# Attention stage of a two-layer trunk: q, k and v tiles paired otherwise, value products with 64 stationary columns, merge factors through DRAM, and the next MLP's first weight splits later

## The chip, the core and the metric

The program runs on one core of a Trainium2 chip. The core has a matrix engine (PE, whose weight loads are listed as PEld), a vector engine (DVE), a scalar engine (ACT), a general engine (POOL) and a queue engine (SP) that issues nearly all DMA transfers. The engines run their own instruction streams in order and wait for each other at semaphores. The metric is the device time of one execution in microseconds (us), lower is better; the kernel before takes 2144.97 us, the median of three runs (2143.05 to 2145.32).

## What is computed

One sequence of 1024 positions with 1024 features goes through two layers in float32. Layer 0 mixes positions with a gated unit in chunks of 128, layer 1 with dilated attention; a squared-ReLU MLP of width 4096 follows each, and norms stand before every block. Only the attention matters here:

```python
for g, (window, dil) in enumerate(((128, 1), (512, 4), (2048, 16))):   # three groups
    s = q_g k_g^T / 8 + bias, banded: a query sees keys t - j*dil, j = 0..window//dil
    m_g = max(s);  p = exp(s - m_g);  den_g = sum(p);  num_g = p @ v_g
m_all = max_g m_g;  c_g = exp(m_g - m_all)
o = sum_g(num_g * c_g) / sum_g(den_g * c_g)     # per head and position
h = h + o @ w_out
```

There are 8 heads of 64 features. The factor that multiplies num_g is c_g divided by the summed denominator: one number per head, position and group.

## The kernel before

**Arithmetic.** A float32 number is split in two parts (`hi`, made by an ACT copy to the float32r type, and `lo`, made by a DVE subtraction, both in `split` at L205 and L206). A product is then three matmuls, hi*hi, hi*lo and lo*hi. Large products use Strassen's scheme with seven block products, numbered 1 to 7 (`seven`, L1189), of 12 matmuls each.

**Stage.** The attention stage takes 36 column blocks of w_qkv, each of 128 columns (two heads): for four head pairs (hp) and three groups (g, in the order 1, 2, 0) a q, a k and a v tile. That makes twelve units U[0] to U[11]. Four tiles come out of a classical product at the start, (0,q), (0,k), (0,v) and (1,q). The other 32 are made in pairs by `seven`; the list `quads` says which two share one call. `put_out(i, s, ...)` hands over half s of the i-th tile of the pair: `out_qk` (L1156) for q and k, which it scales and splits to a hi and a lo tile (L1174 on ACT, L1175 on DVE), `out_v` for v.

**A unit.** For each of four query blocks j of a unit, PE makes scores (12 matmuls with 64 rows, the two heads side by side in the array), DVE adds the bias and takes the maximum (L1270), ACT takes the exponential (L1272), PE transposes the probabilities (`turned`), ACT and DVE split them (L205, L206), and PE multiplies them by V (`values`). In `values` a head's V is 128 stationary columns, the 64 of the hi part beside the 64 of the lo part; two matmuls (by the hi and the lo part of the probabilities) give both halves of the bank, and an ACT copy (L1309) with a DVE addition (L1310) sums the halves into N.

**Merge.** When the third unit (g = 0) of a head pair has its scores for half i of the positions, `merge` computes the factors f on 128 positions x 3 groups x 4 blocks x 2 heads. For each group ACT spreads them over 128 columns per block (L1427), PE transposes them into a bank (`spread_factors`, 4 transposes), and DVE multiplies N by the bank (L1445 for groups 1 and 2, L1456 for group 0). For the first three head pairs the sum goes to DRAM and is read back near the end of the stage; the fourth is split and projected at once.

**What sets the order.** PE's order is the program's own. A planner (`Flow`) runs the projection as the main line, adds up PE time as it issues matmuls, and interleaves generators (attention, v tiles, merges) each of which says with `yield` how many ns later, or after which event, its next PE work is due; the table LAT holds those due times. `flow.until` stops the main line until an event has happened, so the generators' PE work then follows without projection products in between. In `out_qk` the first output of a k tile of unit i stops so until unit i-1 has issued its scores (its tiles need room). The other engines' orders come from a list scheduler, in which `tc.high_priority` pulls work forward.

**Around the end.** After the last pair, `project_three` and `project_last` multiply the merged outputs by w_out, covering the last unit's chain. The next MLP's first weights, `first = [plain(up(1, 0))]`, four loads and four splits of 128 x 512, are issued between the two calls of `project_three`.

Of the kernel before, what the change touches and what calls it, by code (L numbers as in the profile page):

```python
# [10 lines left out]
F32 = mybir.dt.float32  # L11
F32R = mybir.dt.float32r
AF = mybir.ActivationFunctionType
ALU = mybir.AluOpType
# [3 lines left out]
P = 128  # L18
# [89 lines left out]

LAT = dict(sum=2600.0, rms=2600.0, tile=1600.0, gate=8500.0, soft=4700.0, turn=4200.0, fe=1300.0, v=2000.0, qk=4000.0, merge=2600.0, out=700.0, fex=3.0, ve=1600.0)


@with_exitstack
def trunk(ctx: ExitStack, tc: tile.TileContext, xT, w_u, w_v, w_o, w_s, b_s, w_qkv, w_bo, rel,
# [1074 lines left out]

    def seven(w, x, more, put_out, begun=None, first=False):  # L1189

# [19 lines left out]
        if first:  # L1210
            a = one(1)
            u = copied(a)
            d = one(3)
            plus(u, one(6), u)
            one(2, a)
            put_out(0, 0, a)
            e = one(7)
            c22 = plus(u, e)
            f = one(5)
            put_out(1, 1, c22, f, True)  # L1220
            put_out(0, 1, plus(u, f), d, True)
        else:
            u = one(6)
            if begun:
                begun()
            u = copied(u)
            a = one(1)
            plus(u, a, u)
            d = one(5)
            c22 = plus(u, d)  # L1230
            e = one(7)
            put_out(1, 1, c22, e, True)
            one(2, a)
            put_out(0, 0, a)
            one(3, d)
            put_out(0, 1, u, d)
        one(4, e)
        put_out(1, 0, u, e, True)

    def geometry(g, j):  # L1240
# [7 lines left out]
        at = [0, keys[0][1] * P]  # L1248
        return keys, at, at[1] + keys[1][1] * P

    def scores(u, j):
# [11 lines left out]
        for hd in range(2):  # L1263
            p = temp()
            for i in range(2):
# [5 lines left out]
                                               scale=1.0, scalar=BIG, accum_out=m)  # L1271
                nc.scalar.activation(p[:, c], p[:, c], AF.Exp, bias=m, scale=-1.0, accum_out=dn)  # L1272
            ps.append(p)
# [15 lines left out]
    def values(u, j, pts):  # L1289
# [7 lines left out]
        for hd in range(2):  # L1297
            lst = list(parts.items())
            for n, (kb, cs) in enumerate(lst):
                pc, oc, w = cs[0][0], hd * 2 * P + cs[0][1], len(cs) * P  # L1300
                tv, at_ = place(u.g, kb)
                va = u.V[tv][:, at_, 2 * hd:2 * hd + 2, :]
                for e in range(2):
                    matmul(pv[:, oc:oc + w], va, pts[hd][e][:, pc:pc + w], start=(hd == 0 and n == 0 and e == 0),
                           stop=(n == len(lst) - 1 and e == 1), skip_group_check=True)
        for hd in range(2):
            r, x = slice(64 * hd, 64 * hd + 64), slice(64 - 64 * hd, 128 - 64 * hd)
            o, c = u.N[r, 2 * j * P:(2 * j + 2) * P], slice(hd * 2 * P, (hd + 1) * 2 * P)
            nc.scalar.activation(o, pv[x, c], AF.Copy)  # L1309
            nc.vector.tensor_tensor(o, o, pv[r, c], op=ALU.add)  # L1310

# [87 lines left out]
    def merge(hp, i):  # L1399
# [8 lines left out]
        nc.vector.tensor_tensor(mn, mn, e[2][:, :, :, 0], op=ALU.min)  # L1408
        f = small.tile([P, 3, 4, 2], F32, tag="f", name="f", bufs=2)
        for g in range(3):  # L1410
            nc.vector.tensor_tensor(f[:, g], mn, e[g][:, :, :, 0], op=ALU.subtract)
        nc.scalar.activation(f, f, AF.Exp)
        dn = small.tile([P, 4, 2], F32, tag="dn", name="dn", bufs=2)
# [6 lines left out]
        for g in range(3):  # L1420
            nc.vector.tensor_tensor(f[:, g], f[:, g], dn, op=ALU.mult)
        quick.__exit__(None, None, None)
        yield LAT["merge"]
        def factors(g):
# [12 lines left out]
        rest = None  # L1437
        fe_ns = LAT["fe"] * (1.0 if hp == 3 else LAT["fex"])
        early = {g: factors(g) for g in (1, 2, 0)} if hp == 3 else {}
        for g in (1, 2):  # L1440
            fe = early.get(g) or factors(g)
            yield fe_ns
# [5 lines left out]
            else:  # L1448
                nc.vector.tensor_tensor(rest, rest, t, op=ALU.add)
        fe = early.get(0) or factors(0)  # L1450
        yield fe_ns
# [6 lines left out]
        yield LAT["sum"]  # L1458
        if hp < 3:
            if i == 0:  # L1460
                kept_N[hp] = dram.tile([P, S], F32, tag=f"N{hp}", name=f"N{hp}", bufs=1)
            nc.sync.dma_start(kept_N[hp][:, half(i)], N)
        else:
            split_N(hp, i, N)
        merged[hp, i].t = flow.t
# [79 lines left out]
    for n, two in enumerate(quads):  # L1545
# [6 lines left out]
        seven(w, xa, more, lambda i, *x: out(two[i], *x), None if wn else lambda: flow.add(ahead_of_last()), n == 0)  # L1552
        w = wn
# [5 lines left out]
    for m in range(8):  # L1559
        project_three(0, m)  # L1560
    first = [plain(up(1, 0))]
    rest = list(range(8))
    while len(rest) > 4:
        project_three(1, rest.pop(0))
    for i in range(2):
        flow.until(lambda: (3, i) in outs)
        project_last(i, rest if i else ())
        start_terms(sq[i], i, 3, terms)
# [101 lines left out]
```

## Time and profile before

| | |
|---|---|
| median of three runs | 2144.97 us (2143.05 to 2145.32) |
| the profiled execution's own time | 2143.75 us |
| its span, from the first to the last instruction | 2142.0 us |
| PE busy | 2106.6 us, 98% |
| DVE busy | 1640.1 us, 77% |
| ACT busy | 1120.9 us, 52% |
| POOL busy | 566.1 us, 26% |
| mean granted TensorE clock | 0.994 |

Views of the trace give, per stretch of time, the busy time of each engine and the granted clock; per group of equal instructions, their number, busy time and mean duration; per wait, which engine waited for what. In a timeline row stand the start, the time from the first start to the last end, and the instructions with their count. A matmul's row lasts until its result is out, longer than the distance to the next matmul; the price of a matmul in a stream is therefore taken from the starts of rows that follow each other.

### The profile page before, as it was taken

Reading aid. Unit: us, or ns where it says so; the run is one execution under the profiler, and the core shown is the slowest. Engines: PE = TensorE matmul, PEld = TensorE weight load, DVE = VectorE, ACT = ScalarE, POOL = GpSimd, SP = SyncE. Lnnn points to the kernel's source line nnn. Section 1 sums busy time; section 2 is a strip of 40 time slices with the busy share of each in tenths; the row PEclk is TensorE's granted clock in tenths of the full one; section 3 lists DMA queues with packets and bytes.
Section 4 is the critical chain, followed back from the end, with each engine's and each line's share of the span. In section 5 each row is a group of like instructions: output and inputs, shape, how many; then the busy total and the mean of one; then the engine's idle time right before and its main releaser. Section 6 shows DMA issues by size and latency. Waiting matters only on the chain.

```text
span 2142.0 us, 30066 instructions
## 1 busy us (share of the span) xinstructions
PE 2106.6 (98%) x10210; PEld 1745.0 (81%) x10210; DVE 1640.1 (77%) x3014; ACT 1120.9 (52%) x2262; POOL 566.1 (26%) x417
## 2 busy tenths in 40 slices
PE   8999999999999999999999999999999999999998
PEld 7888887888878888887888788887888888888887
DVE  7975268567699888888787877879976666988886
ACT  6644136554564444346666656665555556544433
POOL 2100113233323332531212222101133332432345
PEclk9999999999999999998999999999999999999999
DMA  6411114455354444321112111142155543644432
GB/s 222 142 61 50 40 42 139 157 188 182 128 182 163 158 162 133 94 89 42 46 47 49 40 49 46 47 131 82 39 179 191 188 158 128 196 157 140 144 106 79
DMA packets 158815, 247.04 MB, mean 115 GB/s; under 512 B 33482, under 2 KB 47941, under 8 KB 158661
## 3 DMA queue, kind: packets, MB, share of 16 engines
q1 hardware_dynamic: 158336, 244.94, 35.2%
q8 instruction: 80, 1.31, 0.3%
q14 instruction: 75, 0.61, 0.1%
q10 hardware_dynamic: 324, 0.18, 0.0%
HBM read 180.41 MB, written 64.66 MB: 114 GB/s over the span
## 4 chain that ended last, share of the span: by engine, by line
PE 85%; DVE 9%; ACT 3%; issue 1%; DMA 1%; SPq 0%; DVEq 0%; ACTq 0%
PE at L180 43%; PE mm L180 40%; PE at L187 2%; DVE wp L206 2%; DMA t<-hid 1%; DVE h L340 1%; DVE t L206 1%; ACT t L1272 1%; ACT wp L205 1%; DVE k L1175 0%; DVE q L1175 0%; DVE tr L206 0%; DVE t L1270 0%; DVE N L1310 0%; ACT q L1174 0%
## 5 line engine op out<-in xcount | busy, mean ns | idle before, releaser
L205 ACT ACTIVATE wp<-r 128x512 fp32r<-128x512 f32 (+3 forms) x490 | 294.0, 605 | 455.5 <-PE at L180 287.2
L180 PE MATMUL at<-hx,wp 128*128 128x512 f32 x1770 | 413.7, 389 | 4.6 <-DVE wp L206 2.6
L206 DVE TENSOR_TENSOR wp<-r,wp 128x512 fp32r<-128x512 f32 (+3 forms) x490 | 375.9, 771 | 38.6 <-ACT wp L205 35.0
L180 PE MATMUL mm<-y,wp 128*128 128x512 f32 x1608 | 397.5, 393 | 2.2 <-ACT t L1132 1.0
L180 PEld LDWEIGHTS at<-hx,wp 128*128 128x128 f32 x1770 | 331.7, 188 | 75.8 <-DVE h L940 3.6
L180 PEld LDWEIGHTS mm<-y,wp 128*128 128x128 f32 x1608 | 298.7, 188 | 67.5 <-DVE h L340 1.6
L180 PE MATMUL at<-t,wp 128*128 128x512 f32 x1344 | 314.0, 389 | 0.1
L180 PEld LDWEIGHTS at<-t,wp 128*128 128x128 f32 x1344 | 252.2, 188 | 52.9 <-DVE t L803 0.5
L410 POOL TENSOR_TENSOR t<-r 128x512 f32<-128x512 f32 (+3 forms) x78 | 114.5, 1467 | 678.3 <-DMA r<-in_w_dn 312.7
L412 POOL TENSOR_TENSOR r<-r 128x512 f32<-128x512 f32 (+3 forms) x77 | 116.4, 1512 | 384.9 <-DVE wp L206 352.2
L180 PE MATMUL mm<-t,wp 128*128 128x512 f32 x768 | 195.1, 402 | 0.0
L206 DVE TENSOR_TENSOR hx<-t,hx 128x512 fp32r<-128x512 f32 x192 | 179.8, 949 | 5.7 <-ACT hx L205 5.7
L180 PE MATMUL mm<-hx,wp 128*128 128x512 f32 x708 | 171.7, 389 | 0.0
L180 PEld LDWEIGHTS mm<-t,wp 128*128 128x128 f32 x768 | 143.0, 191 | 30.9 <-issue 0.2
L269 POOL TENSOR_TENSOR t<-t 128x512 f32<-128x512 f32 (+1 forms) x54 | 72.8, 1347 | 347.8 <-ACT t L258 345.9
L180 PE MATMUL mm<-y,whi 128*128 128x512 f32 x512 | 158.1, 390 | 0.0
L180 PEld LDWEIGHTS mm<-hx,wp 128*128 128x128 f32 x708 | 132.7, 188 | 28.1 <-DVE b L966 0.6
L940 DVE TENSOR_TENSOR h<-h,at 128x512 f32<-128x512 f32 x144 | 97.6, 680 | 55.3 <-PE at L180 55.3
L803 DVE TENSOR_TENSOR t<-t,at 128x512 f32<-128x512 f32 x116 | 79.1, 683 | 76.6 <-PE at L180 76.4
L180 PE MATMUL at<-y,wp 128*128 128x512 f32 x552 | 137.5, 390 | 0.0
L205 ACT ACTIVATE hx<-t 128x512 fp32r<-128x512 f32 x192 | 118.4, 628 | 27.7 <-DMA t<-hid 23.3
L415 POOL TENSOR_TENSOR r<-r 128x512 f32<-128x512 f32 (+3 forms) x77 | 105.3, 1368 | 80.9 <-issue 47.1
(225 smaller groups left out, 3187.3 us busy)
## 6 DMA issues: line engine op xcount, KB each, us to landing
t<-hid SPq DMA_DIRECT2D x194, 256.0 KB, 4.9
hid<-t SPq DMA_DIRECT2D x140, 256.0 KB, 2.3
r<-in_w_up SPq DMA_DIRECT2D x128, 256.0 KB, 2.7
r<-in_w_dn SPq DMA_DIRECT2D x88, 256.0 KB, 2.7
r<-in_w_qkv SPq DMA_DIRECT2D x72, 256.0 KB, 2.6
hid<-b SPq DMA_DIRECT2D x56, 256.0 KB, 2.7
r<-in_w_v SPq DMA_DIRECT2D x48, 256.0 KB, 3.6
h<-in_xT SPq DMA_DIRECT2D x16, 256.0 KB, 4.1
```

Source lines behind the costliest of these rows:

```text
L180: nc.tensor.matmul(out, lhsT, rhs, **kw)
L187: nc.tensor.transpose(out, src, ident)
L205: nc.scalar.activation(hi, src, AF.Copy)
L206: nc.vector.tensor_tensor(lo, src, hi.bitcast(F32), op=ALU.subtract)
L269: nc.gpsimd.tensor_tensor(self.acc, self.acc, sq, op=ALU.add)
L340: nc.vector.tensor_tensor(x, x, ps, op=ALU.add)
L410: tt(r7, r[0, 0], r[1, 0], op=ALU.subtract)
L412: tt(r6, r[1, 0], r[0, 0], op=ALU.subtract)
L415: tt(r3, r[0, 1], r6, op=ALU.subtract)
L803: nc.vector.tensor_tensor(out, x, y, op=ALU.add)
L940: engine.tensor_tensor(hs[i, s], hs[i, s], src, op=ALU.add)
L1272: nc.scalar.activation(p[:, c], p[:, c], AF.Exp, bias=m, scale=-1.0, accum_out=dn)
```

## The change

1. **Pairs.** `quads` is ((1,v),(1,k)) and then (i,q),(i,v); (i,k),(i+1,q); (i+1,v),(i+1,k), where it was ((1,k),(1,v)) and then (i,k),(i,q); (i,v),(i+1,q); (i+1,k),(i+1,v). Where the second tile of a pair is a k tile, `seven` keeps the block c22 in its buffer and puts it out last (`hold`). A q tile of unit i from 2 on now stops the main line until unit i-2 has issued its scores; a k tile of unit i still waits for unit i-1. The due time after q and k, LAT["qk"], is 5000 ns in place of 4000.
2. **Value products.** V's hi and lo parts are separate stationary operands of 64 columns; three matmuls (hi*hi, hi*lo, lo*hi) accumulate in 64 partitions of the bank, lo*lo is left out, and one ACT copy per head moves the sum to N. The DVE additions go. The array is addressed in tiles of 128 rows x 64 columns for these matmuls.
3. **Factors.** For three of four head pairs, which are nine of twelve units, the 24 factor columns of a half are transposed at once (128 x 24 to 24 x 128), copied by ACT, written to DRAM as six rows of 512, and read back with a DMA that copies a row to 64 partitions (six per half, two per group). DVE multiplies N by these SBUF tiles. The fourth pair goes as before, its three factor tiles spread early.
4. **Splits.** The next MLP's first weights are issued when the fourth head pair's first half is ready, and their loads not before the last exponential.

```diff
-LAT = dict(... v=2000.0, qk=4000.0, merge=2600.0 ...)
+LAT = dict(... v=2000.0, qk=5000.0, merge=2600.0 ...)
...
-            if m == 1 and i > 0:
-                flow.until(lambda: U[i - 1].scored.t is not None)
+            if m < 1 < i or m and i:
+                flow.until(lambda: U[i - 2 + m].scored.t is not None)
...
-    def seven(w, x, more, put_out, begun=None, first=False):
+    def seven(w, x, more, put_out, begun=None, first=False, hold=False):
...
             f = one(5)
-            put_out(1, 1, c22, f, True)
+            plus(c22, f, c22)
             put_out(0, 1, plus(u, f), d, True)
...
             e = one(7)
-            put_out(1, 1, c22, e, True)
+            if hold:
+                plus(c22, e, c22)
+            else:
+                put_out(1, 1, c22, e, True)
...
         put_out(1, 0, u, e, True)
+        if first or hold:
+            put_out(1, 1, c22)
...
-                va = u.V[tv][:, at_, 2 * hd:2 * hd + 2, :]
-                for e in range(2):
-                    matmul(pv[:, oc:oc + w], va, pts[hd][e][:, pc:pc + w], start=(hd == 0 and n == 0 and e == 0),
-                           stop=(n == len(lst) - 1 and e == 1), skip_group_check=True)
-        for hd in range(2):
-            r, x = slice(64 * hd, 64 * hd + 64), slice(64 - 64 * hd, 128 - 64 * hd)
-            o, c = u.N[r, 2 * j * P:(2 * j + 2) * P], slice(hd * 2 * P, (hd + 1) * 2 * P)
-            nc.scalar.activation(o, pv[x, c], AF.Copy)
-            nc.vector.tensor_tensor(o, o, pv[r, c], op=ALU.add)
+                for v, e in ((0, 0), (0, 1), (1, 0)):
+                    va = u.V[tv][:, at_, 2 * hd + (v + hd) % 2, :]
+                    matmul(pv[0:64, oc:oc + w], va, pts[hd][e][:, pc:pc + w],
+                           start=(hd == 0 and n == 0 and v == 0 and e == 0),
+                           stop=(n == len(lst) - 1 and v == 1), skip_group_check=True)
+        with tc.high_priority(offset=PRIO):
+            for hd in range(2):
+                nc.scalar.activation(u.N[64 * hd:64 * hd + 64, 2 * j * P:(2 * j + 2) * P],
+                                     pv[0:64, hd * 2 * P:(hd + 1) * 2 * P], AF.Copy)
...
+        if hp < 3:
+            yield LAT["merge"] + 1500
+            pt = at_bank()
+            transpose(pt[0:24, 0:P], fs.rearrange("p g n -> p (g n)"))
+            ft = small.tile([24, P], F32, tag="ft", name="ft", bufs=1)
+            rows = dram.tile([6, HALF], F32, tag=f"rows{i}", name=f"rows{i}", bufs=1)
+            with tc.high_priority(offset=PRIO):
+                nc.scalar.activation(ft, pt[0:24, 0:P], AF.Copy)
+            nc.sync.dma_start(rows.rearrange("n (b t) -> (n b) t", b=4), ft)
+            yield 5000
+
+            def row(g):
+                x = temp()
+                for a in range(2):
+                    nc.sync.dma_start(x[64 * a:64 * a + 64, :], rows[2 * g + a:2 * g + a + 1, :].partition_broadcast(64))
+                return x
+
+            pbs = [row(1), row(2)]
+            yield 4000
+            for g, pb in zip((1, 2), pbs):
+                nc.vector.tensor_tensor(own(pb, g), permuted(us_[g].N, i, g), own(pb, g), op=ALU.mult)
+            rest = pbs[0]
+            nc.vector.tensor_tensor(rest, rest, pbs[1], op=ALU.add)
+            pb = row(0)
+            yield 3000
+            yield valued[hp, i], 500
+            N = us_[0].N[:, half(i)]
+            nc.vector.tensor_tensor(N, N, pb, op=ALU.mult)
+            nc.vector.tensor_tensor(N, N, rest, op=ALU.add)
...
-    quads = [((1, 1), (1, 2))]
+    quads = [((1, 2), (1, 1))]
     for i in range(2, NU, 2):
-        quads += [((i, 1), (i, 0)), ((i, 2), (i + 1, 0)), ((i + 1, 1), (i + 1, 2))]
+        quads += [((i, 0), (i, 2)), ((i, 1), (i + 1, 0)), ((i + 1, 2), (i + 1, 1))]
...
-    first = [plain(up(1, 0))]
...
     for i in range(2):
         flow.until(lambda: (3, i) in outs)
+        if i == 0:
+            with tc.issue_after(exps[-1].ins):
+                first = [plain(up(1, 0))]
         project_last(i, rest if i else ())
```

The change moves instructions. Three places are shown; a row is an instruction's line, operation, output and inputs, with the output's shape and the number of equal ones.

The first is PE at the beginning of the attention, inside the first call of `seven`, around the second value products of unit 0. There `at<-k,q` are scores, `at<-tr,V` value products, `at<-ident,t` transposes of probabilities, and `mm<-t_...,wp` products of the projection, three matmuls to a row. Before:

```order
L180 MATMUL at<-k_8538,q_8535 128x256 x2
L180 MATMUL at<-tr,V 128x256 x2
L180 MATMUL at<-tr,V 128x128 x2
L180 MATMUL at<-tr,V 128x256 x2
L180 MATMUL at<-tr,V 128x128 x2
L187 MATMUL at<-ident,t 128x128 x6
L180 MATMUL at<-k_8538,q_8534 128x128 x2
```

With the change:

```order
L180 MATMUL at<-k_8538,q_8535 128x256 x2
L180 MATMUL mm<-t_8764,wp 128x512 x3
L180 MATMUL mm<-t_8767,wp 128x512 x3
L180 MATMUL mm<-t_8770,wp 128x512 x3
L180 MATMUL mm<-t_8773,wp 128x512 x3
L180 MATMUL mm<-t_8776,wp 128x512 x3
L180 MATMUL mm<-t_8779,wp 128x512 x3
L180 MATMUL mm<-t_8782,wp 128x512 x3
L180 MATMUL at<-tr,V 64x256 x3
L180 MATMUL at<-tr,V 64x128 x3
```

Before, scores, value products, transposes and the next scores stood with nothing between them, for three query blocks of unit 0; now 21 projection matmuls stand between the scores and the value products.

The second is SP's queue at the merge of the first head pair. Rows `r<-in_w_qkv` are weight loads, `N_...<-N` stores of a merged half, `t<-bvec` the bias. Before:

```order
L169 DMA r<-in_w_qkv 128x512 x2
L1462 DMA N_10007<-N 128x512
L169 DMA r<-in_w_qkv 128x512 x3
L1071 DMA t<-bvec 64x2x64 x2
L169 DMA r<-in_w_qkv 128x512
L1462 DMA N_10007<-N 128x512
```

With the change:

```order
L1439 DMA rows_10052<-ft 24x128
L1445 DMA t<-rows_10052 64x512 x2
L169 DMA r<-in_w_qkv 128x512 x2
L1445 DMA t<-rows_10052 64x512 x4
L1439 DMA rows_10307<-ft 24x128
L169 DMA r<-in_w_qkv 128x512
L1463 DMA N_10365<-N 128x512
L1445 DMA t<-rows_10307 64x512 x4
L169 DMA r<-in_w_qkv 128x512
L1445 DMA t<-rows_10307 64x512 x2
```

Seven issues per half came into the queue between the weight loads: one store of the six rows and six loads of a row to 64 partitions.

The third is DVE near the end of the stage, where the last unit's probabilities are split (`p<-at,p`) and the fourth pair's merge follows (`t<-N,at`, L1445 before and L1488 now). Before:

```order
L206 TENSOR_TENSOR wp<-r,wp 128x512
L206 TENSOR_TENSOR p<-at,p 128x512
L340 TENSOR_TENSOR h_14011<-h_14011,mm 128x512
L1411 TENSOR_TENSOR f<-mn,st_14036 128x8
L1411 TENSOR_TENSOR f<-mn,ex_13377 128x8
L206 TENSOR_TENSOR p<-at,p 128x512 x2
L1411 TENSOR_TENSOR f<-mn,ex_13834 128x8
L1445 TENSOR_TENSOR t<-N,at 128x512
L206 TENSOR_TENSOR wp<-r,wp 128x512
```

With the change:

```order
L206 TENSOR_TENSOR p<-at,p 128x512 x4
L1426 TENSOR_TENSOR dn<-dn,d_14372 128x8
L206 TENSOR_TENSOR wp<-r,wp 128x512
L1427 RECIPROCAL dn<-dn 128x8
L206 TENSOR_TENSOR wp<-r,wp 128x512
L1429 TENSOR_TENSOR f<-f,dn 128x8 x3
L206 TENSOR_TENSOR wp<-r,wp 128x512 x3
L1488 TENSOR_TENSOR t<-N,at 128x512
L206 TENSOR_TENSOR wp<-r,wp 128x512
```

The splits of the next MLP's first weights (`wp<-r,wp`) now stand behind the last unit's probabilities, close together and among the merge's products.

More of the change, by code (lines that the diff above doesn't have):

```diff
@@ L107 @@
 NT = 11
-LAT = dict(sum=2600.0, rms=2600.0, tile=1600.0, gate=8500.0, soft=4700.0, turn=4200.0, fe=1300.0, v=2000.0, qk=4000.0, merge=2600.0, out=700.0, fex=3.0, ve=1600.0)
+LAT = dict(sum=2600.0, rms=2600.0, tile=1600.0, gate=8500.0, soft=4700.0, turn=4200.0, fe=1300.0, v=2000.0, qk=5000.0, merge=2600.0, out=700.0, fex=3.0, ve=1600.0)
 @with_exitstack
@@ L1422, in merge @@
         quick.__exit__(None, None, None)
+        if hp < 3:
[25 more added lines that the diff above has]
+            nc.vector.tensor_tensor(N, N, rest, op=ALU.add)
+            yield LAT["sum"]
+            if i == 0:
+                kept_N[hp] = dram.tile([P, S], F32, tag=f"N{hp}", name=f"N{hp}", bufs=1)
+            nc.sync.dma_start(kept_N[hp][:, half(i)], N)
+            merged[hp, i].t = flow.t
+            return
         yield LAT["merge"]
@@ L1437, in merge @@
         rest = None
-        fe_ns = LAT["fe"] * (1.0 if hp == 3 else LAT["fex"])
-        early = {g: factors(g) for g in (1, 2, 0)} if hp == 3 else {}
+        fe_ns = LAT["fe"]
+        early = {g: factors(g) for g in (1, 2, 0)}
         for g in (1, 2):
-            fe = early.get(g) or factors(g)
+            fe = early[g]
             yield fe_ns
@@ L1458, in merge @@
         yield LAT["sum"]
[L1459 to L1464, printed above, removed]
+        split_N(hp, i, N)
         merged[hp, i].t = flow.t
@@ L1551, in trunk @@
                 U[i].bias = bias_tile(U[i].hp, U[i].g)
-        seven(w, xa, more, lambda i, *x: out(two[i], *x), None if wn else lambda: flow.add(ahead_of_last()), n == 0)
+        seven(w, xa, more, lambda i, *x: out(two[i], *x), None if wn else lambda: flow.add(ahead_of_last()), n == 0, two[1][1] == 1)
         w = wn
```

11 lines of the change are left out of this document (7 added, 4 removed).

## The prediction

> **What bounds the kernel now.** I read the page's first part, then its clock row, then the chain of waits.
>
> ```profile
> PE 2106.6 (98%) x10210; PEld 1745.0 (81%) x10210; DVE 1640.1 (77%) x3014; ACT 1120.9 (52%) x2262; POOL 566.1 (26%) x417
> PEclk9999999999999999998999999999999999999999
> PE 85%; DVE 9%; ACT 3%; issue 1%; DMA 1%; SPq 0%; DVEq 0%; ACTq 0%
> ```
>
> PE is busy 98% of the span and carries 85% of the chain. So only two things move the time: PE's own work, and the places where PE stands still or runs slowly. The clock row dips once, in slice 19, which is the attention's beginning. Next I cut the stage into its beginning and the rest, with the stretch of the dip by itself (columns: length, PE busy, matmuls, granted clock, DMA share, GB/s).
>
> ```profile
> 973.00:1016.00 43.00, 39.26 (x206) 0.84 0.18 45
> 1016.00:1490.00 474.00, 463.84 (x2755) 1.00 0.21 61
> 990.00:1004.00 14.00, 13.82 (x56) 0.51 0.07 20
> ```
>
> In the first 43 us PE idles 3.7 us, and for 14 us it runs at half the clock, which costs 0.49 * 14 = 6.9 us: 10.6 us lost. In the other 474 us the idle time is 10.2 us. The timeline of PE says why the beginning is bad (start, length, count, idle before).
>
> ```profile
> 985.79 0.82 PE L187 MATMUL at<-ident,t 128*128 128x128 f32 x6
> 986.53 0.96 PE L180 MATMUL at<-k,q 64*128 64x128 f32 x12
> 987.44 0.38 PE L180 MATMUL at<-tr,V 128*128 128x256 f32 x1
> 988.89 1.02 PE L180 MATMUL at<-tr,V 128*128 128x256 f32 x7 [1.06 <-DVE tr L206]
> 990.09 2.06 PE L187 MATMUL at<-ident,t 128*128 128x128 f32 x6 [0.18 <-ACT t L1272]
> 992.07 1.65 PE L180 MATMUL at<-k,q 64*128 64x128 f32 x12
> 993.65 1.97 PE L180 MATMUL at<-tr,V 128*128 128x256 f32 x8
> ```
>
> Scores, transposes and value products of unit 0 follow each other, each waiting for the softmax and splits of the one before; the gap at 987 us stands just ahead of the half clock. The waits of the whole stage (sum, times, longest) are these.
>
> ```profile
> PE at L180 <- DVE tr L206: 3.5, 4, 1.1
> PE at L180 <- DVE q L1175: 2.4, 3, 0.9
> PE at L187 <- ACT t L1272: 1.5, 3, 0.8
> PE at L180 <- DVE V L1123: 1.3, 1, 1.3
> PE at L180 <- ACT q L1174: 0.9, 3, 0.4
> ```
>
> They are short and spread: splits of probabilities, of q and k, of V that come just too late. A busy row counts a matmul to the end of its latency, so a short wait also hides in the row before it; I allow 0.16 us for each of 13 waits, 2 us in all (a 512-column matmul lasts 0.389 us and is followed after 0.227 us, as the next rows show). The rest of the stage thus loses 12.2 us.
>
> **The change, part by part: PE's own work.** The prices of a stream come from starts of rows.
>
> ```profile
> 1160.16 2.20 PE L180 MATMUL mm<-t,wp 128*128 128x512 f32 x9
> 1162.20 1.01 PE L180 MATMUL at<-tr,V 128*128 128x128 f32 x8
> 1163.05 0.62 PE L187 MATMUL at<-ident,t 128*128 128x128 f32 x4
> 1163.60 0.89 PE L180 MATMUL at<-k,q 64*128 64x128 f32 x12
> 1164.41 3.71 PE L180 MATMUL mm<-t,wp 128*128 128x512 f32 x15
> 1167.96 0.84 PE L180 MATMUL mm<-y,wp 128*128 128x512 f32 x3
> ...
> 1465.47 2.92 PE L180 MATMUL at<-p,V 128*128 128x128 f32 x24
> 1468.23 0.62 PE L187 MATMUL at<-ident,t 128*128 128x128 f32 x4
> ```
>
> ```profile
> L180 PE MATMUL at<-t,wp 128*128 128x512 f32 x1344 | 314.0, 389 | 0.1
> ```
>
> Nine matmuls of 512 columns in 2.04 us are 0.227 us each; eight value products in 0.85 us are 0.107 each, 24 others in 2.76 us are 0.115; I use 0.111. A 128-column product streams for a quarter of 0.227, 0.057 us, so the 0.111 is its weight load. A 256-column product streams for 0.113, about as long as the load. Now the array's tile: from 1163.05 to 1167.96 are 4.91 us, in which 4 transposes (0.44), 12 score matmuls that run in pairs (6 * 0.111 = 0.67) and 15 products (3.40) need 4.51. The 0.40 left is the entry into the 64-row tile and the way out: 0.20 each, made of a stream that must run out and of a first weight load that nothing covers.
>
> ```profile
> L180 PEld LDWEIGHTS at<-t,tab 33*8 33x8 f32 x6 | 0.3, 84 | 1.1 <-issue 1.1
> L180 PEld LDWEIGHTS at<-tr,V 128*128 128x128 f32 x388 | 51.4, 193 | 7.7 <-DVE tr L206 2.6 <-DVE V L1123 1.6 <-issue 0.2
> L180 PE MATMUL at<-tr,V 128*128 128x128 f32 x276 | 40.8, 263 | 2.4 <-DVE V L1123 1.3 <-DVE tr L206 1.1
> L180 PE MATMUL at<-tr,V 128*128 128x256 f32 x112 | 25.5, 308 | 1.1 <-DVE tr L206 1.1
> L180 PE MATMUL at<-p,V 128*128 128x128 f32 x28 | 4.2, 261 | 0.0
> L180 PE MATMUL at<-p,V 128*128 128x256 f32 x16 | 3.6, 308 | 0.0
> ```
>
> A load of 8 columns lasts 84 ns and one of 128 lasts 193: 0.9 ns a column. A load of 64 columns should be 58 ns shorter and come every 0.055 to 0.057 us.
>
> *Products.* Before there are 276 + 28 of 128 and 112 + 16 of 256 columns (the 28 and 16 are the last unit's, whose probabilities lie in other tiles): 432 * 0.111 = 48.0 us. With three for two they are 456 and 192: 456 * 0.057 + 192 * 0.111 = 47.3 us. Change -0.7. If a 64-column load were no shorter, the 456 would take 0.111 and the change were +23.9: that is the upper end. I take -0.7, by the row of 8 columns.
>
> *Tile switches.* No row shows a 128 x 64 tile. The 48 blocks of value products now each begin and end with a switch; ten of these 96 fall together with one of the scores, and the six new transposes of 24 columns bring twelve more, 98 in sum. Bounds: nothing, if only the row tile counts, and 0.20 as for scores. The tile of 33 rows and 8 columns changes both and cannot separate them. I take 0.20 for the way out and 0.14 for the way in, whose first load is half as long: 98 * 0.17 = +16.7 us, since nothing makes the one kind of tile better than the other.
>
> The Trainium skill, TensorEngine Tiling (Array Packing), Key Properties, says that a change of the tiling mode, not only of the tile, drains the engine. The scores' 0.20 us agree. By it the switches cost what I took; without it the forecast below would be 16.7 us lower.
>
> *Transposes.* 18 factor tiles of 4 transposes go, six small ones come: -72 * 0.11 + 6 * 0.11 = -7.3 us.
>
> PE's own work: -0.7 + 16.7 - 7.3 = **+8.7 us**.
>
> **Work of the other engines.**
>
> ```profile
> L1310 DVE TENSOR_TENSOR N<-N,at 64x256 f32<-64x256 f32 x96 | 39.7, 417 | 19.4 <-ACT N L1309 18.0
> L1427 ACT ACTIVATE t<-f 128x512 f32<-128x512 f32 x24 | 14.6, 621 | 4.6 <-DVE f L1421 4.6
> L206 DVE TENSOR_TENSOR wp<-r,wp 128x512 fp32r<-128x512 f32 (+3 forms) x490 | 375.9, 771 | 38.6 <-ACT wp L205 35.0
> ex<-sc SPq DMA_DIRECT2D x8, 16.0 KB, 2.4
> sc<-st SPq DMA_DIRECT2D x8, 8.0 KB, 3.4
> t<-bvec SPq DMA_DIRECT2D x8, 256.0 KB, 3.1
> SPq L169 <- DVE wp L206: 284.5, 53, 33.9
> ```
>
> DVE loses 96 additions, 39.7 us, and ACT 18 spreads, 18 * 0.621 = 11.2 us. Neither shows in the time by itself, PE covers both; they shorten the queues in which the splits stand that PE waits for. The merge's way through DRAM has a store (3.4 us for one with small pieces) and a load (3.1 us): 6.5 us beside 9 us of due time, so it is covered if SP is free. SP often is not: its weight loads wait 284.5 us in sum for buffers, and the row loads stand behind some of them. Then the DVE product that needs the row waits, and behind it the scores' maxima and the splits of weights. Bounds: nothing, and 1 us, about a third of a load, at each of the 18 products, 18 us of DVE, which for PE are at most that. I take 1 us, since DVE has more than 39 us to spare by then.
>
> **Stalls.** *Beginning:* the first pair now is v and k with k last, so the main line no longer stops in the middle of unit 0, and PE's order shows 21 projection matmuls, 4.8 us, where the chain stood bare. I take 2 of the 10.6 us as left: -8.6. Bounds: none gained, if the softmax is later than 4.8 us, and all of it. *q and k:* 2.4 + 0.9 us and 1 us in the rows' ends; the longest wait is 0.9 us, and the work is due 1 us later; all but 0.3 goes, -4. *V:* the v tile is made earlier, -1.3 and 0.2 behind it. *Probabilities:* of the waits outside the beginning, 3.5 + 1.5 - 1.2 = 3.8, DVE's lighter queue takes most, -3.5. *Added:* merges +1. At the end, eight weight splits of 0.771 us stand close together on DVE between the last unit's probabilities and its merge, 6.2 us in the chain that the last projection waits for; its 36 matmuls of `project_three` cover most, +2. Sum: -8.6 - 4 - 1.5 - 3.5 + 3 = **-14.6 us**.
>
> The forecast is 2143.75 + 8.7 - 14.6 = 2137.9 us, rounded to **2138**; the profiled execution lies 1.2 us below the median of its three runs, so for a median I would accept up to 2139.
>
> **The rivals.** *No shorter load.* The price of 64 columns is that of 128, and 456 products take 54 ns more each: 2138 + 24.6 = 2162 us, slower. It decides from 0.070 us a product on, where the gain of 6 is gone, and 0.079 makes it slower by 0.2%. The row of 8 columns speaks against it; for it, that no row shows this tile. The Trainium skill, TensorEngine Tiling (Array Packing), Restrictions, has column tiling exclude the fast weight load, which is a way to this rival; the Trainium skill, TensorE: Matmul & The Clock Gate, LDWEIGHTS, gives a plain load as its columns divided by 1.2 in ns, 107 ns for 128, an estimate that the 0.111 us here agrees with, so there seems no fast load to lose.
>
> *The waits move.* The rows come late behind SP's weight loads, DVE stands at 18 products, the end of the stage stands at its eight splits, and of the gain in the stage only the beginning's stays: 2143.75 + 8.7 - 8.6 = 2144 us, no change. For it: DVE executes in order and SP's waits reach 33.9 us. Against it: 39.7 us less on DVE.
>
> *Column tiles switch for nothing.* 16.7 us less: 2121 us. For it: only row tiles are seen to drain. Against it: the scores drain on the way out too, into the full array.
>
> *Stalls stay as they were* although the order changed, because other work is as late: 2143.75 + 8.7 = 2152 us.
>
> **The numbers.** Chances: forecast 0.52, with its own range 2130 to 2145; no shorter load 0.11; the waits move 0.16; free switches 0.14; stalls stay 0.07. The range 2121 to 2153 takes in all but the first rival and the tails. About 0.2%, 4.3 us, is what a measurement of this kernel tells from no change, so faster means below 2140.7 and slower above 2149.3. Faster: 0.14 + 0.45 of the forecast's 0.52 + 0.04 of the moved waits = 0.63. Slower: 0.11 + 0.06 + 0.02 = 0.19. Same: 0.18.
>
> **What would show it.** PE has 10360 matmuls. Value products of 64 columns stand 0.055 to 0.06 us apart where they have 128 moving columns, and their loads last about 0.135 us; 0.19 would be the first rival. At the ends of value blocks 0.14 and 0.20 us are lost; with free switches nothing. The stretch after 973 us has no half clock and about 2 us of idle time; waits for q, k and V are nearly gone. DVE waits for the rows' DMA less than 5 us in all; more than 15 us, with PE waits behind it, is the rival of moved waits. The forecast is wrong above all if the half clock comes back through another gap near the beginning, which alone costs 6.9 us.

## The result and the profile after

The changed kernel takes 2159.88 us, the median of four runs (2157.76 to 2164.08); the kernel before, beside it, 2145.14 (2143.05 to 2145.52). The ratio is 1.0077, 95% interval 1.0065 to 1.0089: slower by 14.7 us between the medians, where 2138 was forecast. The profiled execution of the changed kernel took 2161.28 us, its span 2159.6; that is 17.5 us over the profiled execution before.

First the busy times and the clock row of the changed kernel's page.

```profile
PE 2107.2 (98%) x10360; PEld 1743.4 (81%) x10360; DVE 1607.0 (74%) x2918; ACT 1110.0 (51%) x2251; POOL 561.5 (26%) x417
PEclk9999999999999999999999999999999999999999
```

Then the two stretches of its stage (length, busy time of PE, weight loads, DVE, ACT and POOL with instructions, granted clock, DMA share, GB/s).

```profile
973.00:1016.00 43.00, 39.52 (x240) 31.01 (x239) 33.16 (x82) 30.80 (x83) 12.43 (x8) 1.00 0.13 37
1016.00:1490.00 474.00, 448.56 (x2802) 372.35 (x2801) 338.10 (x860) 275.47 (x742) 72.43 (x52) 0.97 0.24 71
```

The page hardly differs from before; the stretches tell. I count as lost what PE idles, plus what the clock takes: (1 - clock) times the length. The clock has two digits, so the second part is good to 2.4 us in the long stretch.

| us lost | before | after | change |
|---|---|---|---|
| first 43 us: idle + clock | 3.7 + 6.9 | 3.5 + 0 | -7.1 |
| next 474 us: idle + clock | 10.2 + 0 | 25.4 + 14.2 | +29.4 |

Sum +22.3. The execution is only 17.5 us longer, so PE's own work fell by about 5 us; +8.7 was forecast. The whole executions say much the same: PE's idle time went from 35.4 to 52.4 us and the mean clock from 0.994 to 0.992, in sum some 21 us. Both large terms of the forecast are wrong, in opposite directions.

**The beginning** came out as forecast. PE's timeline shows 21 projection products between the scores and the first value products of the stage, and no stretch of half clock follows.

```profile
987.97 0.82 PE L187 MATMUL at<-ident,t 128*128 128x128 f32 x6
988.72 0.95 PE L180 MATMUL at<-k,q 64*128 64x128 f32 x12
989.60 5.05 PE L180 MATMUL mm<-t,wp 128*128 128x512 f32 x21
994.49 1.22 PE L180 MATMUL at<-tr,V 128*64 128x256 f32 x12
```

The new pair is not the only thing that cures it: below, the value products alone, in the old order, already bring the 10.6 us lost here down to 5.7.

**The 64-column tile** is seen in these rows of PE's timeline, with the group of its weight loads.

```profile
1088.11 0.84 PE L180 MATMUL mm<-y,wp 128*128 128x512 f32 x3
1088.79 1.58 PE L180 MATMUL at<-tr,V 128*64 128x128 f32 x18
1090.21 1.06 PE L187 MATMUL at<-ident,t 128*128 128x128 f32 x8
1091.20 0.95 PE L180 MATMUL at<-k,q 64*128 64x128 f32 x12
1092.08 2.33 PE L180 MATMUL mm<-y,wp 128*128 128x512 f32 x9
1094.25 2.88 PE L180 MATMUL mm<-t,wp 128*128 128x512 f32 x12
...
1167.30 0.88 PE L180 MATMUL at<-tr,V 128*64 128x128 f32 x12
1168.01 0.62 PE L187 MATMUL at<-ident,t 128*128 128x128 f32 x4
1168.57 0.89 PE L180 MATMUL at<-k,q 64*128 64x128 f32 x12
```

```profile
L180 PEld LDWEIGHTS at<-tr,V 128*64 128x64 f32 x582 | 50.8, 134 | 5.7
```

Twelve products of 128 moving columns (the row at 1167.30) take 0.71 us, 0.059 each; a load lasts 134 ns. Both as forecast. A row can mix shapes: of the 18 at 1088.79 six have 256 columns, and their 1.42 us leave 0.118 for each of these, where 0.111 was taken. But the switch costs nothing that shows: the three 512-column products ahead of the first value block take 1088.79 - 1088.11 = 0.68 us, which is 3 * 0.227 and no more. On the way out, four transposes ahead of scores take 0.56 us, as before without any column tile (0.55). The scores' row tile still costs: the nine products behind them take 2.17 us in place of 2.04, and the 0.11 to 0.12 us that a group of transposes ahead of scores takes beyond 0.11 for each I read as its way in.

**The stalls** sit at the merges. PE's waits of the changed kernel between 1016 and 1490 us (sum, times, longest):

```profile
PE at L187 <- ACT t L1279: 6.1, 9, 2.2
PE mm L180 <- DVE t L1207: 5.3, 2, 3.2
PE at L180 <- DVE tr L206: 4.8, 3, 3.5
PE mm L180 <- DVE q L1175: 4.6, 2, 2.8
PE at L187 <- ACT t L1470: 2.6, 1, 2.6
```

DVE's wait for the rows in the same stretch:

```profile
DVE t L1451 <- DMA t<-rows: 10.9, 4, 4.4
```

How one merge goes wrong is seen in its timeline, rows of SP, DVE, ACT and PE (start, length, count, idle before).

```profile
1091.34 1.13 SPq L1445 DMA_DIRECT2D t<-rows  x2
1099.71 1.87 SPq L169 DMA_DIRECT2D r<-in_w_qkv  x2
1101.67 2.37 SPq L1445 DMA_DIRECT2D t<-rows  x4
...
1106.59 1.08 DVE L1451 TENSOR_TENSOR t<-N,t 128x512 f32<-128x512 f32 x1 [4.44 <-DMA t<-rows]
...
1107.97 0.40 ACT L1279 ACTIVATE t<-t,st 128x128 f32<-128x128 f32 x1 [6.98 <-DVE st L1277]
...
1111.23 4.24 PE L180 MATMUL mm<-y,wp 128*128 128x512 f32 x12 [3.24 <-DVE t L1207]
1115.27 3.34 PE L180 MATMUL mm<-t,wp 128*128 128x512 f32 x12
```

The first row is loaded at 1091.34. The second is issued 10 us later: two weight loads stand ahead of it in SP's queue, and they wait for a buffer. DVE stands 4.44 us at the second product; behind it in DVE's order are the maximum that ACT waits for and the addition L1207 that frees PE's bank. And the twelve products after PE's 3.24 us gap take 4.04 us instead of 2.72: the gap is paid again in the clock. The granted clock is 0.50 from 1112.8 to 1116.2 us, and 0.94 over the stretch from 1110 to 1140.

### The profile page after: what moved, and what is told of

Read it like the earlier page. It is cut to its first block, busy times and chain, and to the rows that moved or that the text cites. A ratio compares the mean times of both kernels' runs of the same rounds, so it can differ in the third digit from the quotient of the medians.

```text
span 2159.6 us, 30352 instructions
## 1 busy us (share of the span) xinstructions
PE 2107.2 (98%) x10360; PEld 1743.4 (81%) x10360; DVE 1607.0 (74%) x2918; ACT 1110.0 (51%) x2251; POOL 561.5 (26%) x417
```

## The experiments

All differences in us are between medians, to the kernel before run beside it on the same chip (medians 2143.3 to 2144.6).

### The parts alone

The value products alone (`values` of the change in the kernel before):

```diff
-                va = u.V[tv][:, at_, 2 * hd:2 * hd + 2, :]
-                for e in range(2):
+                for v, e in ((0, 0), (0, 1), (1, 0)):
+                    va = u.V[tv][:, at_, 2 * hd + (v + hd) % 2, :]
```

> The value products of 64 columns alone, with the pairing, merge and late start of before. PE's own work goes up by 13.9 us (tile switches), DVE loses 96 additions, 39.7 us. If the lighter DVE queue shortens no stall: 2143.3 + 13.9 = 2157. If it shortens the stalls of before (probabilities, q and k: at most some 9 us outside the half clock): 2148 to 2152. If switches cost nothing: 2143 or less.

2140.36 us, -3.0, ratio 0.9987 (0.9978 to 0.9996): the case "switches cost nothing". Its windows:

```profile
973.00:1016.00 43.00, 39.01 (x239) 30.21 (x238) 32.68 (x85) 31.39 (x83) 9.54 (x7) 0.96 0.16 46
1016.00:1490.00 474.00, 467.08 (x2970) 389.94 (x2969) 351.34 (x893) 294.75 (x773) 82.57 (x58) 1.00 0.20 61
```

It loses 5.7 + 6.9 us in place of 10.6 + 10.2, 8.2 us less, and its profiled execution is 4.8 us shorter: PE's own work grew by some 3 us, not by 14. The 96 additions that DVE no longer makes are the likely reason for the shorter stalls; no run takes them away without the new products. The expectations of these runs counted 13 to 15 us of switches into PE's own work; they rest on the prediction's price and fall with it. Where they say "own work +14" read about +2 (the two prices of the 64-column rows above give +1.6), and where they compare by it, the difference is stall.

The pairing alone (`quads`, the waits in `out_qk`, the held output in `seven`, the due time of 5000 ns):

```diff
-        quads += [((i, 1), (i, 0)), ((i, 2), (i + 1, 0)), ((i + 1, 1), (i + 1, 2))]
+        quads += [((i, 0), (i, 2)), ((i, 1), (i + 1, 0)), ((i + 1, 2), (i + 1, 1))]
```

> The kernel before with the new pairing alone (pairs, held c22, due time 5000, the q tile's stop); value products, factors and splits as before. PE's own work is unchanged. Rows theory (the loss of the whole change comes from the factors' way through DRAM): the beginning gains its 8 to 9 us and later waits some, 2132 to 2138 us. Pairing theory (the new order itself bunches the other engines' work around the g = 0 units): the beginning gains but the later merges lose 10 or more, 2145 to 2155 us.

2162.64 us, +19.3, ratio 1.0091 (1.0074 to 1.0108): beyond both expected ranges. With the later first split of the next MLP beside it (`with tc.issue_after(exps[-1].ins)`):

> The other pairing and the later first split of the next MLP, without the new value products and without the rows: PE's own work is that of before. If the 14 us that the pairing alone loses at the stage's end come from the splits that stand ahead on DVE, they go: 2162.6 - 14 = 2149, or 2144 to 2151; what then is over the 2143.8 of u_rows less its own work (2143.8 - 14.3 = 2129.5) is what the lighter DVE of the new value products gives. If the late start does not matter without the other parts: 2160 to 2164.

2152.51 us, +9.2, ratio 1.0041 (1.0026 to 1.0056), a little over the first expected range. The windows of the pairing alone:

```profile
973.00:1016.00 43.00, 38.87 (x225) 30.24 (x224) 35.66 (x88) 30.51 (x80) 11.59 (x8) 1.00 0.13 38
1016.00:1490.00 474.00, 449.04 (x2681) 377.20 (x2680) 369.94 (x951) 289.52 (x757) 73.02 (x52) 0.98 0.21 61
```

Its longest wait:

```profile
PE at L180 <- DVE N L1315: 9.8, 1, 9.8
```

The windows with both:

```profile
973.00:1016.00 43.00, 38.85 (x225) 30.22 (x224) 35.67 (x89) 30.48 (x77) 11.61 (x8) 1.00 0.14 39
1016.00:1490.00 474.00, 455.00 (x2715) 381.76 (x2714) 379.80 (x966) 292.33 (x765) 71.58 (x52) 0.99 0.20 61
```

The beginning gains, with no half clock, and the rest loses far more. Ten of the 19 us are the last unit's numerator standing on DVE, a single wait of 9.8 us. Behind it the clock is 0.53 from 1453 to 1467 us, another 6.6 us: so some 16 of the 19 are lost at the stage's end. The later split takes the wait away, as the expectation had it, but only 10 us come back; shorter waits stand there instead, 1.8 and 2.5 us just ahead of 1482 and 1485 us.

The rows alone:

> The kernel before with the factors through DRAM alone. PE's own work falls by 6 us (66 transposes less, 11 tile switches more). Rows theory: DVE stands at the factor products for several us in most of the six merges and PE behind it, 2150 to 2160 us. Pairing theory: the old order has room for the rows, 2138 to 2144 us.

2153.19 us, +9.9, ratio 1.004 (1.0025 to 1.0055), although 72 transposes are gone and six small ones came. Its windows:

```profile
973.00:1016.00 43.00, 37.20 (x207) 28.79 (x206) 33.68 (x82) 28.63 (x72) 8.90 (x7) 0.92 0.18 46
1016.00:1490.00 474.00, 459.79 (x2654) 381.56 (x2652) 376.56 (x967) 283.16 (x754) 77.55 (x54) 0.97 0.24 71
```

The rest loses 14.2 us idle and another 14.2 by the clock, against 10.2: in the old order the rows' gaps cost more through the clock than by themselves.

The whole change without the rows, and the whole change without the new value products:

> The whole change without the factors through DRAM: those go by ACT spread and transposes as before. PE's own work is 14 us over the kernel before (87 tile switches more, transposes kept). Rows theory: 2143 to 2150 us, as the stalls fall by 9 to 16. Pairing theory: still 2158 or more, since it pays the 14 and the bunching.

> The whole change with the value products of before (full width, with DVE's addition): PE's own work is 6.4 us below before and 14.7 below the whole change; DVE has 39.7 us more work than the whole change. If the additions stand in DVE's queue together with the factor products (DVE-order theory), the stalls grow by much of what the own work saves: 2155 to 2170. If the 64-column tiles' switches are simply the dearer and DVE's load does not matter: 2160 - 14.7 = 2145.

Without rows 2143.81 us, +0.5, ratio 1.0001 (0.9992 to 1.0011); without the value products 2165.17, +21.9, ratio 1.0102 (1.0085 to 1.0119). So the rows bring the 14 us between u_rows and the whole change, some 20 with the 6 us or so of transposes that they save, and the value products take 7 us off the rest. The windows without rows:

```profile
973.00:1016.00 43.00, 39.54 (x239) 31.17 (x239) 33.12 (x83) 30.88 (x83) 12.42 (x8) 1.00 0.13 35
1016.00:1490.00 474.00, 461.49 (x2938) 386.04 (x2937) 349.51 (x885) 294.09 (x766) 76.85 (x55) 0.99 0.21 61
```

The rest loses 12.5 idle and some 4.7 by the clock, against 10.2 before and 6.9 with the value products alone: what the beginning gains, 7 us, the new pairs give back.

### Why the rows cost

Two kernels relieve one suspect each, a third relieves both: the row loads issued from POOL's queue (`nc.gpsimd.dma_start` at L1445), the factor products and sums on POOL (`nc.gpsimd.tensor_tensor` at L1451 to L1459), and both.

> The whole change, but the row loads are issued from POOL's queue and so do not stand behind SP's weight loads. Queue theory (a form of the rows theory: the row load is late because SP waits for a weight buffer): DVE's waits for rows fall from 10.9 to under 3 us and the time to 2145 to 2152. If the row loads are late because their destination buffers come free late, or the loss is elsewhere, it stays at 2157 to 2163.

> The whole change, but the five factor products and sums of each of the six halves (the two factor rows times the numerators, their sum, the local row times its numerator, the last sum) run on POOL instead of DVE. PE's own work is that of the whole change. Theory A (the rows cost time because these products stand in DVE's in-order queue ahead of the splits and bank additions that PE waits for): about 22 us of the whole change's 2160 go, so that only PE's shorter work against u_rows is left, 2135 to 2143; PE's waits for DVE's probability splits, q and terms fall under half of theirs. Theory B (the rows cost time through SP's queue and through row buffers that come free late, wherever the products run): 2150 to 2160, with POOL waiting for the rows' DMA in place of DVE.

> The whole change, with the row loads issued from POOL's queue (not behind SP's weight loads) and the factor products and sums on POOL (not in DVE's order), both at once. Each alone took 3 to 5 us of the 16 to 22 that the rows cost. Theory Q (two in-order queues cover for each other, and with one of them relieved the other one still stands): 2136 to 2146. Theory T (the rows hold three of the eleven temporary buffers for 10 to 20 us a half, and DVE, ACT and SP wait for those buffers, wherever loads are issued and products run): 2150 to 2158.

2155.04 us (+11.7), 2157.43 (+14.1) and 2167.91 (+23.3). The first takes 3 us off, the second almost none, both together make it worse: neither order alone is the cause. 2155.04 has the ratio 1.0056 (1.0041 to 1.0071), 2157.43 has 1.0065 (1.005 to 1.008), 2167.91 has 1.011 (1.0096 to 1.0124); the first two intervals overlap with that of the whole change, 1.0065 to 1.0089, and the first and the third time lie outside both ranges that were expected. In the first, DVE's wait for the rows falls from 10.9 to 3.6 us, as its queue theory had it, and most of the loss stays. The other two are no clean relief: a factor product that takes DVE 1.07 us takes POOL 1.56. With both, DVE waits for POOL's factor work; its waits from 1016 to 1490 us:

```profile
DVE q L1175 <- POOL t L1451: 12.4, 2, 6.2
DVE t L1277 <- POOL t L1453: 9.9, 2, 5.0
```

And one row of DVE's timeline in that kernel:

```profile
1106.85 0.29 DVE L1277 CUSTOM_DVE_ANT_0 t<-at,b 128x128 f32<-128x128 f32 x1 [4.93 <-POOL t L1453]
```

The maximum at L1277 reads nothing that the merge makes. It writes a temporary `t`, and waits for L1453, the last reader of the second row's: it waits for the buffer. All softmax tiles, splits and rows share the 11 buffers of `temp()`. Two tests of that:

```diff
-NT = 11
+NT = 10
```

> The whole change without the rows (2143.8), with 10 temporary buffers in place of 11, in the whole program. It takes away the resource that theory T names, without rows, without DMAs and without added work. Theory T: the attention stage loses time with one buffer less, 1016 to 1490 us gets 4 us or more of PE idle time beyond u_rows' 12.5, and the whole program 2149 to 2165. Theory Q: buffers are no limit, 2143 to 2146.

2160.51 us, +15.9, ratio 1.0077 (1.0062 to 1.0093), against +0.5 with eleven. One buffer fewer costs as much as the rows do, with no row in the kernel: the eleven leave nothing to spare. That the rows' loss is this one, it doesn't show by itself. Its window:

```profile
1016.00:1490.00 474.00, 451.41 (x2881) 377.69 (x2880) 341.55 (x870) 288.19 (x760) 75.19 (x53) 0.98 0.21 60
```

And an ACT wait for a temporary that the merge's sum frees, in the same stretch. With eleven buffers there is none at this line; the only wait for that sum is at the spreads (L1434), 10.3 us, which with ten is 7.6:

```profile
ACT t L1201 <- DVE t L1456: 12.0, 2, 6.0
```

The other test holds one row at a time (value products and old pairing; rows loaded singly from POOL's queue, products written into the numerators in place):

> The value products of 64 columns with the old pairing, and factors through DRAM in a form that holds one row buffer at a time: rows loaded one after the other from POOL's queue, each product written into the numerators in place, no buffer for their sum. PE's own work is 6 us below a_val. Theory T: with one buffer held at a time, most of the 6 us shows, 2135 to 2139. If rows cost by their lateness whatever they hold: 2145 to 2156.

2148.84 us, +4.2, ratio 1.0022 (1.0013 to 1.0031). It misses the buffer theory's range: 7 us over a_val, each to its own kernel before, so rows cost even when few buffers are held. A direct relief, more buffers for the changed kernel, wasn't tried.

### The loads taken apart

Into the kernel without rows I put the rows' loads alone, at the same places of the program as in the whole change, in steps. u_hold: three temporaries a half loaded by six DMAs from SP and touched by five DVE operations of 8 columns (30 in the trace; the expectations below count six a half and 36). u_queue: the same into small tiles of their own.

```diff
+            x = temp()
+            for a in range(2):
+                nc.sync.dma_start(x[64 * a:64 * a + 64, :], xT[2 * g + a:2 * g + a + 1, 0:HALF].partition_broadcast(64))
...
+            nc.vector.tensor_tensor(x[:, 0:8], x[:, 0:8], y[:, 0:8], op=ALU.add)
```

> The whole change without the rows (u_rows, 2143.8), and beside its old merge the rows' loads alone: at the times of the whole change three temporary buffers a half are loaded with two broadcast DMAs each from SP's queue, and held until DVE touches 8 columns of them (6 operations of 8 columns a half in place of products of 512). No product moves. Theory T (held buffers): most of the rows' 16 to 22 us of stalls returns, 2155 to 2165. If the products in DVE's order were what costs: 2144 to 2149.

> As u_hold, but the loads go to three small tiles of 32 columns of their own, so that no temporary buffer is held; the same number of DMAs from SP's queue at the same times, the same touches on DVE. Theory T: 2143 to 2148, no more than the DMAs' issue and SP's order cost. If SP's queue (weight loads behind row loads) is what costs: 2150 to 2160.

u_hold 2167.62 us, +23.8, ratio 1.0104 (1.0089 to 1.0119), a little over its theory's range: no product is needed for the loss. u_queue (2151.89, +8.1) tells nothing: its loads depend on no merge, and its trace shows them between 8 and 90 us of the program. The next two bind them to the merge by a small array that each merge writes first; the second leaves DVE's touches out.

> u_queue's loads read an input and were placed in the first 100 us, so they told nothing of the merges. Here they read a small array in DRAM that each merge writes from its factors first (one store and six broadcast loads of 24 columns a half from SP's queue, then six small touches on DVE), so they cannot come earlier; they go to three small tiles of their own, no temporary buffer is held. Theory T (held buffers): 2143 to 2149, with the 12.5 us of PE idle time of u_rows in 1016 to 1490. If SP's queue and DVE's order are what costs: 2152 or more.

> As u_queue2 (the same store and six loads a half from SP's queue into small tiles), but nothing reads the loaded tiles: the 36 small operations on DVE are left out, so DVE never waits for a load. If u_queue2's 13.9 us over u_rows are DVE standing in its order for the loads (13.7 us of DVE waits there): 2143 to 2148. If they are SP's queue, weight loads behind stores and row loads: 2153 to 2158.

u_queue2 2157.66 us, +14.0, ratio 1.007 (1.0053 to 1.0087); u_queue3 2147.33, +4.0, ratio 1.0018 (1.0008 to 1.0028). The window of the rest, first u_hold's, then u_queue2's, then u_queue3's:

```profile
1016.00:1490.00 474.00, 446.93 (x2832) 373.30 (x2831) 333.13 (x885) 283.04 (x751) 74.76 (x52) 0.98 0.24 69
```

```profile
1016.00:1490.00 474.00, 453.35 (x2897) 379.24 (x2895) 341.70 (x897) 286.79 (x754) 71.73 (x52) 0.99 0.22 62
```

```profile
1016.00:1490.00 474.00, 459.81 (x2933) 384.90 (x2931) 345.02 (x880) 293.19 (x767) 75.64 (x54) 0.99 0.22 62
```

DVE's wait for the loads in u_queue2, in the same stretch:

```profile
DVE dq L1417 <- DMA dq<-rows: 13.7, 16, 1.6
```

My buffer theory (T in the expectations) as I had it expected u_queue2 near 2146, and falls as the only cause. The steps are: +0.5 without loads, +4.0 with the loads in SP's queue, +14.0 when DVE also reads them in its order, +23.8 when they hold temporaries too. So in these kernels the store and loads in SP's queue cost some 3.5 us, at the edge of the noise, and DVE standing for the landing 10; these two steps change nothing else. The last 10 are not shown to be held buffers alone: u_hold's loads are also longer, 512 columns for 24, follow no store, and come later. The first merge's loads go out from 1092.6 us on in u_hold, as in the whole change (1091.3), and from 1074.1 in u_queue2. In the whole change the sum is about 20; how the three divide in it stays open, and the relief of SP's queue with its 3 us says that the parts don't simply add up.

### A version that beats both

The value products, and the new order in the first pair alone (a_val with these lines; the output of the first k is put out last, as in the change):

```diff
-    quads = [((1, 1), (1, 2))]
+    quads = [((1, 2), (1, 1))]
```

> The value products of 64 columns and only the first pair of projections in the new order (v, then k); all later pairs, the merge and the start of the next MLP as before. If the new pairing helps at the stage's beginning alone and costs in the later pairs: the first 43 us lose 3.5 us as with the whole change (a_val: 4.0 idle and 4% of the clock), so 2 us less than a_val's 2140.4, 2136 to 2139. If the beginning's gain needs the later pairs: 2140 to 2144.

2138.47 us, -6.2, ratio 0.9972 (0.9962 to 0.9983). Its windows:

```profile
973.00:1016.00 43.00, 39.98 (x242) 31.44 (x241) 33.58 (x84) 31.35 (x83) 11.00 (x8) 1.00 0.17 45
1016.00:1490.00 474.00, 467.03 (x2973) 389.68 (x2972) 352.98 (x893) 294.17 (x772) 80.24 (x57) 1.00 0.21 61
```

It loses 3.0 + 7.0 us, half of the 20.8 before: the beginning's gain needs one pair only, and the rest keeps its old order. Of the 10.8 us, 8.2 are gone with the value products alone; the intervals of the two kernels overlap.

## Why the prediction was wrong, step by step

- **Tile switches, +16.7: the first step that failed.** Measured about zero: 0.68 us for the three products ahead of a block, 0.56 for the transposes behind one. I took the scores' price for the new tile "since nothing makes the one kind of tile better than the other"; my lower bound was the truth, and the rival of free switches had the mechanism. The Trainium skill, TensorEngine Tiling (Array Packing), Key Properties, has a change of mode drain the array: the trace agrees for the 64-row tile and differs for the 64-column tile, where the measurement decides.
- **Products -0.7 and transposes -7.3** held in the mechanism, with the 10360 matmuls that were counted. The sizes are a little off: 0.059 us for 0.057 and 0.118 for 0.111 add 2.3 us to the products, and own work is about 5 us lower where the two terms make 8.
- **Beginning, -8.6:** the size held, -7.1, and there is no half clock; 3.5 us are idle where I left 2. The cause held in part: the pairing alone cures the half clock, but the value products alone, which the term does not name, take 4.9 us of it too.
- **q and k -4, V -1.5, probabilities -3.5:** failed. Even without rows the rest of the stage loses 17 us, where these terms were to leave 3 of 12. The pairs did not remove waits, they moved them: the pairing alone costs 19 us, some 16 of them at the stage's end. The relief that did come, 3.3 us in the rest, came with the value products (a_val) and is the size credited to DVE's additions, 3.5.
- **Merges, +1: the step that decided.** Measured about +20. The mechanism was named, a row load behind SP's weight loads and DVE standing at the product, but it was sized as 18 short waits that 39 us of freed DVE time would absorb, and its upper bound let PE lose no more than DVE waits. DVE waited 10.9 us for the rows, between the two marks of 5 and 15 that the prediction had set, and PE lost about twice that. What counts is not an engine's spare total, but what stands behind the wait at that moment: the maxima, the bank additions, and, as far as the runs with ten buffers and with held ones tell, the eleven buffers that I did not count at all. And a gap of PE is paid a second time in the clock, 14 us here beside 25 of idle time.
- **End of the stage, +2:** the size is about right (2.6 us at the last merge's transposes), by luck: there PE waits for ACT's spread, which stands behind ACT's copies of weights whose load is late, and not for DVE's splits. Half a clock from 1484.8 to 1488.2 us adds 1.7. The run of the pairing alone shows the end with the splits left early.

The rival "the waits move" had the place and was priced at the gain it cancels, 2144, as if a moved wait could only take back what had been won. The two large errors are about -14 in PE's work and +37 in stalls. The range took the rivals one at a time; with the merges' own upper bound of 18 us added to the stalls that stay, 2152, it would have reached the result.

## What to carry to other kernels

When a value goes from an engine to another through DRAM, count three things beside the DMA's time: what stands ahead of the load in its queue, what stands behind the reader in its engine's order, and for how long the landing buffer is taken out of a shared ring. A test of the ring is cheap: run the kernel with one buffer fewer. When PE is 98% busy, a change that frees another engine's time can win a little (a_val, 0.13%) even where it adds PE instructions, and an order that cures one gap should be applied to that gap alone first.

## What the runs showed that I had not expected

A 64-column tile follows a full one and is followed by one without loss, while a 64-row tile costs 0.11 to 0.13 us on each side beyond the instructions' prices in the rows above. Weight loads of 64 columns let products of 128 moving columns follow each other each 0.059 us, where 0.111 was taken from the kernel before. The clock's price of gaps: 25.4 us of idle time in the long stretch came with a granted clock of 0.97, which is 14 us more, while 10.2 us in the kernel before came with 1.00. The sum of the idle time does not set that price: 14.2 us with the rows alone came with 0.97 as well, and 25.0 with the pairing alone with 0.98.
